# Merge gates of a streaming encoder layer: dense tiles, or pairs in seven quarter products added up in DRAM

## The chip, the cores and the metric

The kernel runs on one core of a Trainium2 chip. The metric is the device time of one launch in microseconds (us). One launch does one layer for a prompt of 1024 frames and a sample of 32 frames; the two are laid side by side, so that most operations work on T = 1056 columns.

## The reference, cut to what matters

```
h = rms(x);  z = h @ w_in, split into [q,k,v,r of the linear attention (GLA) | q,k,v of the band attention | gates gA, gB]
A = GLA(q, k, v) -> per-head rmsnorm, * silu(r), @ w_br_a          (4 heads)
B = softmax attention over a band of chunks, @ w_br_b              (8 heads)
mix = (sigmoid(gA)*A + sigmoid(gB)*B) @ w_out;   x += rms(mix)
x += rms(ConvFFN(rms(x)));   x += rms(sigmoid(rms(x) @ w_ple_gate) * (p @ w_ple))
```

The change concerns `z = h @ w_in`, with 1024 rows of h (the features) and 6672 columns of z. A *tile* is 128 of these columns: `Q0, K0, V0, R0` are the first tiles of the linear attention's q, k, v, r, `QB0, KB0, VB0` those of the band's, `GA0` and `GB0` those of the merge gates (8 tiles each). A tile's result has 128 partitions and T columns.

## The kernel before

Everything is kept in float32 accuracy by splitting each operand into a high and a low part (`whi`, `wlo` for weights, `xh`, `xl` for the normed input, 8 blocks of 128 rows each). A product of two such operands is three matmuls per block: high by high, high by low, low by high.

There are two ways to compute tiles of z. A *dense* tile is done in three chunks of 352 columns, 24 matmuls each, so 72 matmuls of 128x352. A *pair* of tiles in `in_strassen` takes the 2 by 2 form of Strassen and Winograd: the weights of both tiles are cut into quarters of four blocks, the input into quarters of four blocks by half of T (`one`, `two`), and seven quarter products replace eight. Each quarter product is 24 matmuls of 128x264, so a pair is 168 of them. It needs sums of weight quarters (made on VectorE) and sums of input quarters, named `t1` to `t4`, which were split into tiles `th` and `tl` at the start and live in SBUF until the stage of pairs ends.

The stages of the program, in order: start and norms; the stage of pairs (10 pairs: r, gB, and the first half of gA); the band attention; a short change-over; the linear attention in 16 steps `u` (4 heads by 4 segments); then the branch products, FFN and the rest, which the change touches only in where gates get their sigmoid. Inside the attentions the dense tiles that are left (`tiles`, 29 of them) are *fill*: TensorE has little work of its own there, so the code puts `piece()` between its steps. A piece is a third of a chunk, 8 matmuls on average. `flush()` writes the evacuations of finished chunks (PSUM to SBUF on ScalarE), `split_half` splits the next weights. TensorE, VectorE and ScalarE run in the written order (`manual_schedule`); on the DMA queues of SP and POOL a scheduler sets the order.

In the linear attention PSUM gives two banks to `mm` (fill) and six to `one`. A step turns the keys (`key_turns`, `key_copies`), forms products on six levels, masks them into `scores`, turns these (`score_turn` writes `turned`), updates the state, makes the outputs, and normalises them one step later (`roots`, `output_copies`, `output_turns`). `weight_sum` and `branch_sum` let POOL's queue add weight quarters of later stages in DRAM: a one-element DMA as a marker, a copy, and an accumulating DMA.

## Time and profile before

| what | before |
|---|---|
| median of 3 runs | 1871.55 us (1870.84 to 1872.83) |
| the profiled execution: its time / span of its records | 1871.93 / 1870.2 us |
| TensorE (PE) busy | 1841.6 us, 98% |
| VectorE (DVE) / ScalarE (ACT) / GpSimd (POOL) busy | 1287.3 / 976.9 / 227.7 us |
| stage of pairs | 81.7 to 287 us |
| band attention, change-over | 287 to 591 us |
| linear attention, up to its last step | 591 to 845 us |
| moved by DMA | 337.08 MB |

The profile is one execution. Matmuls are pipelined, so their recorded durations overlap, and an engine's busy time is the union of them. The pace of TensorE is therefore read from the distance of successive starts, not from the durations. A line such as `L822` is a line of the kernel's source.

### The profile page before, as it was taken

The page shows a single profiled execution, that of the slowest core. Times are in us where ns is not written, and L with a number is a line of the kernel's source. Part 1 is how long each engine was busy: PE and PEld are TensorE (multiplying, and loading weights), DVE is VectorE, ACT ScalarE, POOL GpSimd, SP SyncE. Part 2 cuts the span into 40 slices and gives each one's busy share as a digit, 9 for nine tenths or more (in the row PEclk, how much of TensorE's full clock was granted, in tenths as well). Part 3 has the DMA queues.
Part 4 walks back from the last instruction along what each step waited for, and adds up shares of the span by engine and source line. Part 5 has one row for each costly group of instructions (what it writes and reads, how often), then busy time and mean ns, then how long its engine had stood idle before and what let it go on. Part 6 is the DMA issues. An engine that isn't in the chain of part 4 may idle for free.

```text
span 1870.2 us, 35172 instructions
## 1 busy us (share of the span) xinstructions
PE 1841.6 (98%) x13808; PEld 1805.7 (97%) x13808; DVE 1287.3 (69%) x2427; ACT 976.9 (52%) x2062; POOL 227.7 (12%) x426
## 2 busy tenths in 40 slices
PE   8999999999999999999999999999999999999997
PEld 8999999999999999999999999999999999999996
DVE  6955543656655766766847776888888875568776
ACT  7545334666666676653536455433333345555555
POOL 0000001131100111100010121112122211000112
PEclk9999999999999999999999999999999999999998
DMA  7222326355434656678685477554566679887746
GB/s 283 85 104 100 120 81 198 96 142 139 118 84 123 163 151 181 165 213 268 235 252 174 155 266 283 169 177 169 182 183 172 166 212 303 287 273 248 234 150 111
DMA packets 129905, 337.08 MB, mean 180 GB/s; under 512 B 15236, under 2 KB 40652, under 8 KB 129100
## 3 DMA queue, kind: packets, MB, share of 16 engines
q1 hardware_dynamic: 93020, 221.82, 36.0%
q0 software_dynamic: 35280, 108.34, 22.0%
q10 hardware_dynamic: 1440, 4.69, 0.6%
q8 instruction: 108, 1.77, 0.4%
q14 instruction: 57, 0.47, 0.1%
HBM read 226.53 MB, written 133.29 MB: 192 GB/s over the span
## 4 chain that ended last, share of the span: by engine, by line
PE 85%; DVE 5%; ACT 4%; DMA 4%; issue 2%; SPq 0%; ACTq 0%; DVEq 0%
PE two L2387 6%; PE two L2385 6%; PE two L2386 6%; PE mm L822 5%; PE mm L824 5%; PE mm L823 5%; PE two L617 4%; PE two L618 4%; PE two L619 4%; PE mm L229 3%; PE mm L231 3%; PE mm L230 3%; PE two L2832 3%; PE two L2830 3%; PE two L2831 3%
## 5 line engine op out<-in xcount | busy, mean ns | idle before, releaser
L822 PE MATMUL mm<-xh,whi 128*128 128x352 f32 x696 | 240.5, 346 | 0.8 <-ACT ev L713 0.8
L824 PE MATMUL mm<-xh,wlo 128*128 128x352 f32 x696 | 225.0, 323 | 0.0
L823 PE MATMUL mm<-xl,whi 128*128 128x352 f32 x696 | 224.6, 323 | 0.0
L2832 PE MATMUL two<-d,wlo 128*128 128x264 f32 x616 | 174.4, 283 | 1.3 <-DVE wlo L2566 1.3
L2831 PE MATMUL two<-d,whi 128*128 128x264 f32 x616 | 174.7, 284 | 0.2 <-DVE d L2517 0.2
L2830 PE MATMUL two<-d,whi 128*128 128x264 f32 x616 | 174.6, 284 | 0.0
L2375 ACT ACTIVATE whi<-ws 128x512 fp32r<-128x512 f32 x88 | 55.5, 632 | 161.7 <-PE two L2386 160.7
L822 PEld LDWEIGHTS mm<-xh,whi 128*128 128x128 f32 x696 | 131.1, 188 | 3.3 <-ACT ev L713 1.1
L823 PEld LDWEIGHTS mm<-xl,whi 128*128 128x128 f32 x696 | 131.4, 189 | 0.0
L824 PEld LDWEIGHTS mm<-xh,wlo 128*128 128x128 f32 x696 | 130.6, 188 | 0.0
L2386 PE MATMUL two<-ml,whi 128*128 128x264 f32 x448 | 126.5, 283 | 0.0
L2387 PE MATMUL two<-mh,wlo 128*128 128x264 f32 x448 | 125.9, 284 | 0.0
L2385 PE MATMUL two<-mh,whi 128*128 128x264 f32 x448 | 125.8, 283 | 0.0
L2832 PEld LDWEIGHTS two<-d,wlo 128*128 128x128 f32 x616 | 116.4, 189 | 1.8 <-DVE wlo L2566 1.8
L2831 PEld LDWEIGHTS two<-d,whi 128*128 128x128 f32 x616 | 115.8, 188 | 0.5 <-DVE d L2517 0.5
L2830 PEld LDWEIGHTS two<-d,whi 128*128 128x128 f32 x616 | 115.7, 188 | 0.0
L235 DVE TENSOR_TENSOR wlo<-raw,whi 128x512 fp32r<-128x512 f32 x80 | 54.7, 688 | 59.3 <-ACT whi L234 58.8
L618 PE MATMUL two<-tl,whi 128*128 128x264 f32 x320 | 90.8, 284 | 0.0
L617 PE MATMUL two<-th,whi 128*128 128x264 f32 x320 | 90.8, 284 | 0.0
L619 PE MATMUL two<-th,wlo 128*128 128x264 f32 x320 | 90.6, 284 | 0.0
L2566 DVE TENSOR_TENSOR wlo<-wraw,whi 128x512 fp32r<-128x512 f32 (+1 forms) x81 | 51.7, 644 | 50.1 <-ACT whi L2565 50.0
L2386 PEld LDWEIGHTS two<-ml,whi 128*128 128x128 f32 x448 | 84.2, 188 | 0.0
(778 smaller groups left out, 6267.1 us busy)
## 6 DMA issues: line engine op xcount, KB each, us to landing
raw<-in_w_in SPq DMA_DIRECT2D x52, 512.0 KB, 3.7
d_b<-av POOLq DMA_DIRECT2D x33, 528.0 KB, 3.4
d_ws<-in_w_down POOLq DMA_DIRECT2D x24, 704.0 KB, 6.6
uraw<-d_b SPq DMA_DIRECT2D x32, 528.0 KB, 5.8
raw<-in_w_up SPq DMA_DIRECT2D x29, 512.0 KB, 4.6
sraw<-in_w_up SPq DMA_DIRECT2D x22, 512.0 KB, 3.6
wraw<-d_ws SPq DMA_DIRECT2D x16, 704.0 KB, 6.0
d_b<-sm POOLq DMA_DIRECT2D x11, 792.0 KB, 6.0
```

What stands on the lines that cost most here:

```text
L617: pe.matmul(ps[:, j, :HC], w[0][:, k], x[0](k, s), start=st, stop=False, skip_group_check=True)
L618: pe.matmul(ps[:, j, :HC], w[0][:, k], x[1](k, s), start=False, stop=False, skip_group_check=True)
L619: pe.matmul(ps[:, j, :HC], w[1][:, k], x[0](k, s), start=False, stop=sp_, skip_group_check=True)
L822: pe.matmul(ps, wh, h[:, k, s], start=(k == 0), stop=False)
L823: pe.matmul(ps, wh, l[:, k, s], start=False, stop=False)
L824: pe.matmul(ps, wl, h[:, k, s], start=False, stop=(k == cnt - 1))
L2385: pe.matmul(ps[:, j, :HC], w[0][:, k], x[0][:, k, s], start=st, stop=False, skip_group_check=True)
L2386: pe.matmul(ps[:, j, :HC], w[0][:, k], x[1][:, k, s], start=False, stop=False, skip_group_check=True)
L2387: pe.matmul(ps[:, j, :HC], w[1][:, k], x[0][:, k, s], start=False, stop=sp_, skip_group_check=True)
L2830: pe.matmul(o, wh, xh_[:, s], start=(k == 0 and p in (0, 4, 5)), stop=False, skip_group_check=True)
L2831: pe.matmul(o, wh, xl_[:, s], start=False, stop=False, skip_group_check=True)
L2832: pe.matmul(o, wl, xh_[:, s], start=False, stop=(k == HD - 1 and p in (3, 4, 6)), skip_group_check=True)
```

## The change

It trades places. The 16 gate tiles leave the stage of pairs and the dense fill, and become fill of a new kind: 8 pairs (tile n with tile n+4, `GATES`) of seven quarter products each, one product at a time, inside the change-over and the linear attention. Ten pairs of other tiles take the vacated places in the stage of pairs: r as before, three of band k with v, one of two band q tiles, k with q and the two v tiles of head 0. Thirteen dense tiles are left.

A quarter product is half an `Item`: two pieces of 12 matmuls of 128x264. The half results are not joined in SBUF: ScalarE copies each from PSUM to a staging tile `fv`, and POOL's queue writes or adds it to the gates' rows in DRAM (`into`), 72 DMAs in all. In the chained items the second half goes on accumulating in the bank that was just copied out. Since the input sums no longer fit in SBUF, they are stored to DRAM during the stage of pairs (`sum_store`) and later loaded over quarters of `xh`/`xl` that are no longer needed (`place`). The weight sums of the gates are made in DRAM too (`gate_sum`, 32 of them). The sigmoid of the gates moves to where they are read; for the tiles n below 4 the second half is stored with the opposite sign, so its sigmoid has scale -1.

Further: results of dense tiles and of the new pairs go through DRAM and are loaded where they are used (`band_row`, `head_value`, `head`); `weight_sum` moves from the linear attention to the band attention, and the accumulating DMAs of both sums are held back by two places (`second_sum`); the low halves of weights are written after the next piece begins (`lows`), `tidy` writes all evacuations but the last before each piece; `score_turn` moves ahead of two groups of exponentials; the pieces are spread by counts (`BAND_PIECES`, `GLA_FIRST`, `slot`) instead of `need`.

The core of the diff:

```diff
+BAND_PIECES = 120
+GLA_FIRST = 126
...
+    def gate_sum(n, at):
+        p, i = divmod(n, 4)
+        o = d_gs[p, i]
+        po.dma_start(o[0:1, 0, 0:1], at)
+        po.dma_start(o, (gate_quarter(p, 1, 0), d_gs[p, 0], gate_quarter(p, 0, 0), d_gs[p, 1])[i])
+        po.dma_start(o, gate_quarter(p, *((1, 1), (0, 0), (1, 0), (0, 1))[i]), accum_op=ALU.add)
...
     for n in range(0, 8, 2):
         in_strassen(R0 + n, R0 + n + 1, AF.Silu, d_sr[n], d_sr[n + 1], G_GLA + n)
-    for w0, d, top in ((GB0, d_gb, 8), (GA0, d_ga, GA_DENSE)):
-        for n in range(0, top, 2):
-            in_strassen(w0 + n, w0 + n + 1, AF.Sigmoid, d[n], d[n + 1])
+    for hp in (1, 2, 3):
+        in_strassen(KB0 + hp, VB0 + hp, None, d_bt[hp, 0], d_bt[hp, 2], keep=hp)
+    in_strassen(QB0 + 1, QB0 + 2, None, d_bt[1, 1], d_bt[2, 1], scale=(0.125, 0.125))
+    in_strassen(K0, Q0, None, d_kq[0, 0], d_kq[0, 1], scale=(1.0, QS))
+    in_strassen(V0, V0 + 1, None, d_v[0], d_v[1])
...
-    tiles = gate_tiles[:1] + [t for hp in (1, 2, 3) for t in band_tiles(hp)] + head_tiles(0) + gate_tiles[1:2]
-    tiles += [t for h in (1, 2, 3) for t in head_tiles(h)] + gate_tiles[2:]
+    tiles = [(QB0 + 3, keeper(d_bt[3, 1], 0.125))]
+    for h in (1, 2, 3):
+        tiles += [(K0 + h, keeper(d_kq[h, 0], 1.0)), (Q0 + h, keeper(d_kq[h, 1], QS))]
+        tiles += [(V0 + 2 * h + j, keeper(d_v[2 * h + j], 1.0)) for j in range(2)]
+    for p in range(0, 8, 2):
+        tiles.append(Item(False, *[(gate_quarter(q, 0, 1), 1, Q21, 1.0, into(False, (GATES[q][2], one))) for q in (p, p + 1)]))
+    for p, (n1, n2, z1, z2) in enumerate(GATES):
+        tiles.append(Item(True, (gate_quarter(p, 0, 0), -1, Q11, -1.0, into(True, (z1, one))),
+                          (d_gs[p, 1], 1, Q12, 1.0, into(False, (z2, one), (z2, two), (z1, two)))))
...
+    def item_parts(i, c):
+        half, j = divmod(c, 2)
...
+        if not (half and x.chain):
+            fill["banks"][j] = ps_mm()[:, :HC]
+        ps = fill["banks"][j]
...
+        def evac():
+            if j == 0:
+                fill["stage"] = stage_tile()
+            t = fill["stage"]
+            ac.activation(t[:, j * HC : (j + 1) * HC], ps, AF.Copy, scale=scale)
+            if j:
+                store(t)
```

Three places in the program show what stands in the engines' rows. In the rows a name with a number is one buffer, `out<-in` its operands, and a wait names the engine or DMA lane whose semaphore is awaited.

TensorE, in the step of the linear attention that begins head 1, ahead of the state update (`kt` are the turned keys, `whi` and `wlo` split weights, `mm` the fill's bank, `ot` the outputs of the step ahead). Before:

```order
L822 MATMUL mm_7783<-xh_111,whi_7638 128x352
L823 MATMUL mm_7783<-xl_112,whi_7638 128x352
L824 MATMUL mm_7783<-xh_111,wlo_7639 128x352
L1375 MATMUL one_7811<-vt_6951,kt_7806 128x256 [waits PE_49,Activation_49]
L1375 MATMUL one_7811<-vt_6951,kt_7806 128x256
L1320 MATMUL one_7727<-x_7570 128x128 [waits DVE_49]
L1320 MATMUL one_7728<-x_7570 128x128 [waits DVE_49]
L1462 MATMUL one_7825<-ident_78,ot_7735 128x128 [waits Activation_49]
```

The same place after:

```order
L1440 MATMUL one_8073<-x_7906 128x128 x2
L859 MATMUL mm_8108<-xh_108,whi_8058 128x264 [waits Activation_49]
L860 MATMUL mm_8108<-xl_109,whi_8058 128x264
L861 MATMUL mm_8108<-xh_108,wlo_8059 128x264 [waits DVE_49]
```

The fill ahead of the update is now the second half of a chained item: its first matmul waits for ScalarE, which must have copied out the same bank, and its third for VectorE's low part of the weights.

ScalarE at the same place, from the turned keys on (`fv` is a staging tile, `kq` the keys and queries of the next head). Before:

```order
L1343 ACTIVATE kt_7806<-one_7731 128x256
L1455 ACTIVATE ot_7735<-one_7717,rs_7760 128x256 [waits DVE_49]
L1455 ACTIVATE ot_7735<-one_7717,rs_7760 128x256
L1455 ACTIVATE ot_7735<-one_7605,rs_7760 32x256
L742 ACTIVATE kq_7764<-mm_7783 128x256 [waits DMAHW1_49,DMAHW0_49,PE_49]
L742 ACTIVATE kq_7764<-mm_7783 128x96
L1261 ACTIVATE x_7770<-x_7770 128x64x2 [waits DMASW4_49,DVE_49]
```

After:

```order
L867 ACTIVATE fv_8131<-mm_8108 128x264 [waits DMASW7_49,PE_49]
L867 ACTIVATE fv_8131<-mm_8136 128x264 [waits PE_49]
L1340 ACTIVATE vt_7158<-one_8162 128x512 [waits PE_49]
L817 ACTIVATE whi_8182<-raw_7916 128x512 [waits DMAHW2_49]
L1465 ACTIVATE kt_8185<-one_8077 128x256
L1577 ACTIVATE ot_8081<-one_8063,rs_8127 128x256 [waits DVE_49]
L1577 ACTIVATE ot_8081<-one_8063,rs_8127 128x256
L1577 ACTIVATE ot_8081<-one_7942,rs_8127 32x256
L867 ACTIVATE fv_8230<-mm_8108 128x264 [waits DMASW1_49,DMASW2_49,DMASW0_49,PE_49]
L867 ACTIVATE fv_8230<-mm_8136 128x264 [waits PE_49]
```

Two evacuations of an item and a weight split stand ahead of the keys' copy, two more evacuations behind it, and an evacuation waits for POOL's DMAs (the lanes DMASW) that last read its staging tile.

POOL in the linear attention (`d_ws` and `d_gb` are in DRAM). Before:

```order
L1490 DMA d_ws_6827<-x_7570 1x1 [waits DMASW0_49,DVE_49,Activation_49]
L1491 DMA d_ws_6827<-d_ws_6827 16x11264 [waits DMASW0_49]
L1492 DMA d_ws_6827<-in_w_down 128x1408 [waits DMASW1_49]
L1490 DMA d_ws_6827<-x_7770 1x1 [waits DMASW3_49,DVE_49,Activation_49]
L1491 DMA d_ws_6827<-d_ws_6827 16x11264 [waits DMASW3_49]
```

After:

```order
L748 DMA d_gb_964<-fv_7433 128x528 [waits DMASW1_49,Activation_49]
L748 DMA d_gb_964<-fv_7498 128x528 [waits DMASW2_49,Activation_49]
L748 DMA d_gb_964<-fv_7498 128x528 [waits DMASW3_49]
L748 DMA d_gb_964<-fv_7498 128x528 [waits DMASW4_49]
L774 DMA xl_109<-fv_7569 1x1 [waits DMASW5_49,Activation_49]
L748 DMA d_gb_964<-fv_7569 128x528 [waits Activation_49]
L775 DMA xl_109<-d_t_960 128x4x528 [waits DMASW7_49,DMASW5_49]
```

Where the queue added weights of a later stage, it now stores the gates' quarter products, and loads the input sums behind a marker; the weight sums stand in the band attention's rows.

More of the change, by code (lines that the diff above doesn't have):

```diff
@@ L182, in width @@
         return CHUNKS[c][1] - CHUNKS[c][0]
-    def rstd(s, rows=P):
-        c, a = next((c, a) for c, (a, b) in enumerate(CHUNKS) if a <= s.start and s.stop <= b)
-        return rstds[c][:rows, s.start - a : s.stop - a]
     convst = tl(cst, [P, FT, 2], tag="convst")
@@ L807, in times_gate @@
         return evac
+    def item_parts(i, c):
+        half, j = divmod(c, 2)
+        x, (src, sign, (rows, cols), scale, store) = tiles[i], tiles[i].halves[half]
+        h, l = [t[half] for t in fill["w"][i]]
+        if not (half and x.chain):
+            fill["banks"][j] = ps_mm()[:, :HC]
+        ps = fill["banks"][j]
+        s = slice(cols.start + j * HC, cols.start + (j + 1) * HC)
+        for k in range(HK):
+            b = rows.start + k
+            pe.matmul(ps, h[:, k], xh[:, b, s], start=(k == 0 and not (half and x.chain)), stop=False, skip_group_check=True)
+            pe.matmul(ps, h[:, k], xl[:, b, s], start=False, stop=False, skip_group_check=True)
+            pe.matmul(ps, l[:, k], xh[:, b, s], start=False, stop=(k == HK - 1), skip_group_check=True)
+        def evac():
[5 more added lines that the diff above has]
+                store(t)
+        fill["done"].append(evac)
+        yield
     def unit_parts(i, c):
+        if isinstance(tiles[i], Item):
+            yield from item_parts(i, c)
+            return
         hi, lo = fill["w"][i]
@@ L1517, in emit @@
     head(1)
-    while fill["at"] < 3 * 15 + 1:
+    while fill["n"] < GLA_FIRST:
         piece()
@@ L1542, in steps_of, with slot @@
             f()
-    need = [fill["at"] + n / 30 for n in range(82, 82 * 12 + 1, 82)]
-    need += [3 * FIRST - (3 * FIRST - need[-1]) * n / 3 for n in (2, 1)]
+    slots = [0]
+    def slot(k=1):
+        for i in range(k):
+            slots[0] += 1
+            if OB.get("h") is not None or fill["n"] < min(MAIN, GLA_FIRST + (MAIN - GLA_FIRST) * slots[0] / (9 * 14.7)):
+                piece()
     level_start(0)
@@ L1643, in emit @@
             gate_rows(1)
+        if u == 15:
+            log_exp()
         roots(u)
-        if u < 14 and fill["at"] + (fill["now"] or (0, 0))[1] / 3 < need[u]:
-            piece()
+        flush()
+        if u < 15:
+            gates(u)
+        if u < 14:
+            slot()
         if u == 13:
```

322 lines of the change are left out of this document (197 added, 125 removed).

## The prediction

> **What bounds the kernel now.** I read the page's engines first, then the stages by windows, then who TensorE waits for, and last the pace of its matmuls.
>
> ```profile
> PE 1841.6 (98%) x13808; PEld 1805.7 (97%) x13808; DVE 1287.3 (69%) x2427; ACT 976.9 (52%) x2062; POOL 227.7 (12%) x426
> PE 85%; DVE 5%; ACT 4%; DMA 4%; issue 2%; SPq 0%; ACTq 0%; DVEq 0%
> ```
>
> TensorE is busy for 98% of the span and carries 85% of the chain that ended last. By stage (columns: length, then busy time and count of PE, weight loads, DVE, ACT, POOL, then granted clock, DMA share, GB/s):
>
> ```profile
> 81.70:287.00 205.30, 204.55 (x1680) 204.34 (x1680) 110.42 (x163) 88.91 (x122) 1.09 (x6) 1.00 0.29 99
> 313.00:575.00 262.00, 258.04 (x1779) 246.08 (x1779) 156.79 (x386) 167.29 (x403) 39.57 (x90) 1.00 0.44 112
> 575.00:592.00 17.00, 17.00 (x114) 16.74 (x114) 6.98 (x22) 11.99 (x41) 0.27 (x1) 1.00 0.48 151
> 592.00:852.00 260.00, 259.56 (x1647) 245.30 (x1646) 183.37 (x541) 165.61 (x605) 30.72 (x53) 1.00 0.64 176
> 852.00:881.00 29.00, 28.23 (x169) 26.06 (x168) 17.20 (x48) 10.09 (x27) 0.83 (x1) 1.00 0.82 257
> 881.00:986.00 105.00, 105.00 (x817) 104.84 (x815) 74.32 (x119) 47.30 (x80) 5.12 (x6) 1.00 0.78 251
> ```
>
> These are the pairs, the band attention, the change-over, the linear attention, its end and the branch stage. No stage leaves TensorE idle by more than 4 us at full clock, so time falls where matmul columns fall, as long as the other engines keep up. Who it waits for from 287 to 592 us, then from 592 to 905 us (total us, times, longest):
>
> ```profile
> PE two L954 <- DVE sm L960: 1.9, 4, 0.6
> PE one L967 <- ACT s L961: 1.3, 8, 0.2
> PE mm L822 <- ACT ev L713: 0.8, 1, 0.8
> PE one L1008 <- DVE pt L970: 0.7, 1, 0.7
> PE mm L822 <- DVE ev L804: 0.6, 1, 0.6
> PE one L1219 <- ACT ev L713: 0.4, 1, 0.4
> ```
>
> That is 4.7 us in 14 waits, 0.34 us each, and then 1.0 us: the fill covers nearly every delay of the attentions.
>
> **Fewer columns.** The pace of matmuls by successive starts, first of the pairs (35 starts in this stretch), then of dense fill (96 starts):
>
> ```profile
> 199.80 0.29 PE L619 MATMUL two<-xh,wlo 128*128 128x264 f32 x1
> 203.94 0.28 PE L617 MATMUL two<-th,whi 128*128 128x264 f32 x1
> 287.12 0.32 PE L822 MATMUL mm<-xh,whi 128*128 128x352 f32 x1
> 302.55 0.32 PE L824 MATMUL mm<-xh,wlo 128*128 128x352 f32 x1
> ```
>
> 4.14 us over 34 steps is 0.1218 us for 264 columns; 15.43 us over 95 is 0.1624 us for 352. Sixteen dense tiles' worth of work leaves: 16 x 72 x 0.1624 = 187.1 us. Eight pairs come: 8 x 168 x 0.1218 = 163.7 us. The stage of pairs keeps its ten pairs. So TensorE sheds **23.4 us**, all of it fill. By place: up to the linear attention there were 46 chunks of 24 matmuls (179.3 us) and will be 13 tiles and 9 of the new pieces (152.0 + 13.2 = 165.2 us), 14.1 us less; in the linear attention 41 chunks (159.8 us) become 103 pieces of 12 x 0.1218 = 1.46 us (150.5 us), 9.3 us less.
>
> The Trainium skill speaks against this: TensorE: Matmul & The Clock Gate, section Back-to-back issue gap, gives for a sustained stream of weight loads and matmuls about 81 ns at 128 columns and 131 ns at 512, so narrow matmuls pay more per column. An estimate on a straight line between these is 99 ns at 264 and 110 ns at 352; by it a pair costs 16.6 us against 15.9 us for two dense tiles, and the change would add 5.7 us instead of taking 23.4. The rows above decide otherwise: 0.1218 to 0.1624 is as 264 to 352 in both widths, so I give that outcome no chance.
>
> **More work for ScalarE and VectorE in the linear attention.**
>
> ```profile
> L234 ACT ACTIVATE whi<-raw 128x512 fp32r<-128x512 f32 x80 | 49.5, 623 | 16.2 <-PE mm L823 8.9 <-PE two L618 7.2
> L713 ACT ACTIVATE ev<-mm 128x352 f32<-128x352 f32 x69 | 31.3, 454 | 23.7 <-PE mm L824 22.1 <-issue 1.1
> L1343 ACT ACTIVATE kt<-one 128x256 f32<-128x256 f32 x16 | 6.0, 377 | 0.5 <-PE one L1338 0.5
> L235 DVE TENSOR_TENSOR wlo<-raw,whi 128x512 fp32r<-128x512 f32 x80 | 54.7, 688 | 59.3 <-ACT whi L234 58.8
> 650.80:669.00 18.20, 18.20 (x112) 16.52 (x111) 12.10 (x36) 8.91 (x34) 1.90 (x3) 1.00 0.53 136
> 669.00:686.00 17.00, 17.00 (x113) 16.53 (x111) 11.07 (x32) 14.37 (x49) 1.88 (x3) 1.00 0.56 150
> 686.00:703.20 17.20, 17.20 (x113) 16.75 (x111) 12.78 (x40) 11.30 (x44) 1.90 (x3) 1.00 0.54 146
> L1297 PE MATMUL one<-kq x72: 206/326/430, 590.9 to 845.2; 128*128 128x192 f32 x64, 128*32 128x48 f32 x8
> ```
>
> A dense tile costs ScalarE two weight splits and three evacuations, 2 x 0.623 + 3 x 0.454 = 2.61 us. An item, with half a tile's matmuls, costs two splits and four evacuations of 264 columns; the nearest row for those is the keys' copy, 0.377 us: 2.75 us. In the linear attention 13.67 tiles (35.7 us) become 25.75 items (70.9 us): ScalarE rises from 165.6 to about 201 us of a stage that would last 251, 80%. VectorE gains 2 x 0.688 us for each item more: 183.4 + 16.6 = 200 us, 80% too. The last row gives the first and last step's start: 15 steps in 254.3 us, 16.95 us each. The three rows above it are steps of the second head; the fullest has 14.37 us of ScalarE, and with 35.2 / 15 = 2.3 us more it holds 16.7 us, against a step that should shrink by 9.3 / 15 to 16.3. So the throughput just holds in most steps, but the margins go. One of the rows shown above goes with it: a wait of 0.34 us. I take one such wait in each of 16 steps, **+5.4 us**. Bounds: 0 (ScalarE still idles 50 us there, and `score_turn` now stands ahead of exponentials), and 16 us, half a ScalarE split and evacuation (0.5 of 1.0 us) twice in each step.
>
> **The change-over.** From 575 to 592 us there were 27 dense first matmuls (81 in all, 13.2 us); now 6 new pieces, 8.8 us. So 4.4 of the 23.4 us shed lie here, and could leave 12.6 us, which ScalarE's 11.99 us nearly fill. Here the cover goes, and the exponentials of the first step are late next. I take a third as not won, **+1.5 us** (0 to 4.4).
>
> **Sigmoids.** Eight gate rows more get theirs after the pairs.
>
> ```profile
> L1797 ACT ACTIVATE ev<-ev 128x1056 f32<-128x1056 f32 x4 | 4.3, 1082 | 1.3 <-DMA ev<-d_ga 1.3
> L652 ACT ACT_TABLE_LOAD x2 | 2.6, 1283 | 0.3 <-DVE ev L651 0.3
> 859.30 0.28 ACT L1330 ACTIVATE turned<-one 128x128 f32<-128x128 f32 x1 [4.51 <-PE one L1329]
> 875.00 0.63 ACT L234 ACTIVATE whi<-raw 128x512 fp32r<-128x512 f32 x1 [7.00 <-PE mm L823]
> ```
>
> Four stand in the last step: 4 x 1.08 us and two table loads of 1.28 us, 6.9 us on ScalarE, where it idled 4.5 us at the last step's turn and 7.0 us after. One load stands ahead of the last `roots`, which the output turns wait for: **+0.5 us** (0 to 2.6). The others lie beside the branch stage, where ScalarE is busy for 47 of 105 us: 0 (to 1).
>
> **DMAs and their queues.** POOL's list grows by 174 rows, SP's by 88.
>
> ```profile
> q1 hardware_dynamic: 93020, 221.82, 36.0%
> q0 software_dynamic: 35280, 108.34, 22.0%
> raw<-in_w_in SPq DMA_DIRECT2D x52, 512.0 KB, 3.7
> d_tb<-ev POOLq DMA_DIRECT2D x6, 528.0 KB, 7.8
> gw<-d_gate POOLq DMA_DIRECT2D x4, 1024.0 KB, 11.1
> 712.07 0.84 POOL L1492 DMA_DIRECT2D d_ws<-in_w_down  x1 [5.01 <-DMA d_ws<-d_ws]
> POOL bias L895 <- DMA bias<-in_rel: 122.0, 7, 29.5
> ```
>
> POOL moved 108.34 MB in 22% of the span, 411 us of all engines, 263 MB per ms. In the stage of pairs, 32 weight sums of two times 256 KB and 16 stores of 528 KB are 25 MB, 96 us: the share goes from 0.29 to about 0.76. Weights land in 3.7 us and are asked for a pair (20.5 us) ahead, so 0 (to 3). In the band attention 16 weight sums move in, 32 x 704 KB or 23 MB, 88 us of 250, and about 12 MB of stores and loads of q, k, v at SP's 329 MB per ms, 36 us: 0.44 becomes 0.94. POOL's `bias` fills (L895) stand behind these sums; POOL waited 122 us there for data and has a whole half-head, 262 / 8 = 33 us, to be late. **+1 us** (0 to 6). In the linear attention 72 gate stores need an issue of 0.84 us each in 250 us, and an accumulating store of twice their size lands in 7.8 us while a staging tile is free for three others; a sum's load takes 11.1 us and is issued at least 9 pieces (20 us) ahead: 0 (to 3).
>
> **Sum**: -23.4 + 5.4 + 1.5 + 0.5 + 1.0 = -15.0 us against the execution's own 1871.9 us, which is 0.4 us above the median: 1856.9, and 1856.5 against the median. With all low ends: 1848. A change of 0.2%, 3.7 us, is about what a measurement can tell from none.
>
> **The rivals.**
> - *All of it hidden* (0.14): ScalarE's 50 us of slack and the new order cover every delay; even some of the 4.7 us before the linear attention may go. 1848. For it: TensorE waited 1.0 us there before. Against: 80% occupancy on two in-order engines.
> - *ScalarE sets the steps* (0.13): the upper bound of that term, 16 us, eats most of the gain: 1871.5 - 23.4 + 16 + 3 = 1867, so half of it lies within 0.2%. For it: 16.7 us of ScalarE in a step of 16.3. Against: the steps beside the full one have 8.9 and 11.3 us, so what is late can be caught up.
> - *The two banks* (0.08): this one ends slower. Each half of a chained item adds to the bank that ScalarE has just copied out, with one other piece between; before, a bank rested for three pieces. With the other 3 us of cost, the gain of 23.4 is gone if the 112 new pieces wait 0.18 us each; with one split (0.62) and an evacuation (0.38) ahead at every third piece the mean is 0.33 us, 37 us in all: 1871.5 - 23.4 + 37 + 3 = 1888. For it: six instructions stand between two evacuations in ScalarE's new rows. Against: the own work of the linear attention stands between most pieces. The Trainium skill, Perfetto Trace Analysis, section Matmuls, asks for independent groups to rotate through different banks so that an evacuation overlaps the next group; no run so far shows its price here.
> - *DMA in the band attention* (0.05): at a share of 0.94 the band's own loads come late, say 4 us in each of 7 half-heads: 1871.5 - 15 + 28 = 1884. Against: the branch stage runs at 0.78 without a wait.
> - Two of these at once (0.02): slower.
>
> **How the numbers follow.** The forecast's case has 0.58 and reaches by itself from 1849 to 1864, the term of waits at 0 or 13 us. The predicted time is 1856.5. From 1847 to 1872 hold this case, most of the hidden one and the one of ScalarE, 0.83. Faster by over 0.2%: 0.58 + 0.14 + half of 0.13, 0.78; within: the other half, 0.07; slower: 0.08 + 0.05 + 0.02 = 0.15.
>
> **What will show it.** The new fill's matmuls at 0.122 us from start to start; the stage of pairs within 2 us of 205; the linear attention's 15 steps at 16.3 to 16.8 us each; ScalarE near 200 us there. Waits of fill on `fv` of more than 0.2 us a piece would show the two banks; waits of L954's successor on DMAs the band. It would be wrong if the steps stayed at 17 us, which I would see as waits on ScalarE's splits or evacuations.

## The result, and the profile after

The change made the kernel slower: 1897.9 us median (1889.7 to 1902.5, 4 runs) against 1871.2 us for the kernel before beside it, a ratio of 1.0138 (95% interval 1.0102 to 1.0174). The forecast was 1856.5 us.

The profiled execution took 1898.3 us, its span is 1896.4 us, 26.2 us more than the span before. Three rows per kernel say where. The first start of the row `one<-kq` is the start of the linear attention, its last start that of the last step; the first weight sum of the FFN (`ws<-sraw`) comes after the branch stage. The row `one<-kq` of before stands in the prediction (590.9 to 845.2); these are the sum of before, and both rows of after:

```profile
L2368 DVE TENSOR_TENSOR ws<-sraw x22: 683/684/694, 1170.9 to 1490.3; 128x512 f32<-128x512 f32 x22
```

```profile
L1417 PE MATMUL one<-kq x72: 206/326/401, 610.2 to 867.0; 128*128 128x192 f32 x64, 128*32 128x48 f32 x8
...
L2504 DVE TENSOR_TENSOR ws<-sraw x22: 684/688/694, 1196.9 to 1516.2; 128x512 f32<-128x512 f32 x22
```

| part | before | after | change | forecast |
|---|---|---|---|---|
| up to the linear attention | 590.9 | 610.2 | +19.3 | -14.1 + 1.5 + 1.0 = -11.6 |
| its 15 steps | 254.3 | 256.8 | +2.5 | -9.3 + 5.4 = -3.9 |
| last step to the FFN's first weights | 325.7 | 329.9 | +4.2 | +0.5 |
| the rest | 699.3 | 699.5 | +0.2 | 0 |
| sum | 1870.2 | 1896.4 | +26.2 | -15.0 |

Of the 41.2 us between forecast and result, 30.9 lie ahead of the linear attention, 6.4 in its steps, 3.7 behind them. Windows of after (columns as in the prediction: length, busy time and count of PE, weight loads, DVE, ACT, POOL, then granted clock, DMA share, GB/s), for the pairs, the band and the linear attention:

```profile
81.70:286.90 205.20, 204.50 (x1681) 204.29 (x1682) 110.35 (x163) 80.23 (x115) 79.47 (x127) 1.00 0.80 228
313.00:575.00 262.00, 236.62 (x1601) 225.86 (x1600) 143.22 (x354) 153.87 (x372) 68.63 (x136) 0.95 0.85 231
610.20:867.00 256.80, 251.48 (x1876) 235.95 (x1875) 191.92 (x553) 187.15 (x648) 59.75 (x88) 1.00 0.87 236
```

In the stage of pairs the DMA share went from 0.29 to 0.80 and TensorE did not notice: 205.2 us against 205.3. In the band attention it went from 0.44 to 0.85, and TensorE is idle for 25 us of the same 262, where it was idle for 4. Who it waited for from 287 to 610 us:

```profile
PE one L1188 <- DMA qs<-d_alr: 14.7, 1, 14.7
PE two L1035 <- DVE sm L1041: 8.6, 5, 5.3
PE mm L859 <- ACT fv L867: 2.2, 2, 1.4
PE mm L890 <- ACT fv L734: 2.0, 1, 2.0
```

Two of these waits, 14.7 and 5.3 us, are most of it. The first is for the low-rank input of the gates (`qs<-d_alr`), which `decays` asks for through POOL's queue. POOL's timeline shows when it got there (start, duration of the issue, in brackets what it waited for before):

```profile
544.71 0.56 POOL L1139 DMA_DIRECT2D d_wa<-in_w_br_a  x1 [19.59 <-DMA d_wa<-sums]
545.26 0.50 POOL L1155 DMA_DIRECT2D d_ws<-d_ws  x1
549.77 0.83 POOL L1132 DMA_DIRECT2D d_wa<-in_w_br_a  x1 [4.01 <-DMA d_wa<-in_w_br_a]
551.27 0.84 POOL L1132 DMA_DIRECT2D d_ws<-in_w_down  x1 [0.66 <-DMA d_ws<-d_ws]
551.80 0.86 POOL L1183 DMA_DIRECT2D qs<-d_alr  x1
```

The load is issued at 551.8 us, behind the last weight sums, on a queue that had just stood 19.6 us for a marker of one element. In the kernel before it was issued at 536.8 us and landed in 3.8 us, here in 9.8; so 15 us of its lateness come from the queue's order and 6 from its own landing. TensorE stands from 547 to 561.8 us. The other wait starts on SP's queue and ScalarE:

```profile
514.48 0.30 SPq L1175 DMA_DIRECT2D d_inv<-ot  x1
```

```profile
536.64 0.38 ACT L1055 ACTIVATE ot<-one 64x256 f32<-64x256 f32 x1 [6.65 <-DMA d_inv<-ot]
```

A store of 9 KB, issued at 514.5 us, let its tile go 22 us later; ScalarE stood in order for that tile, the scores' exponentials behind it, VectorE behind these, TensorE behind VectorE. Behind both stand late landings, seen in the DMA issues from 286 to 592 us (KB of each, median us from issue to landing), before and after:

```profile
raw<-in_w_in SPq DMA_DIRECT2D x15, 512.0 KB, 3.6
bias<-in_rel SPq DMA_DIRECT2D x8, 336.0 KB, 2.8
d_wa<-sums POOLq DMA_DIRECT2D x16, 0.0 KB, 1.5
```

```profile
d_ws<-in_w_down POOLq DMA_DIRECT2D x24, 704.0 KB, 15.0
raw<-in_w_in SPq DMA_DIRECT2D x10, 512.0 KB, 14.9
bias<-in_rel SPq DMA_DIRECT2D x8, 336.0 KB, 11.0
d_wa<-sums POOLq DMA_DIRECT2D x16, 0.0 KB, 12.2
```

These three land four to eight times later, on SP's queue as on POOL's; most others land 1.5 to some three times later (`kl<-kl` 8.3 and 12.2 us, `kh<-kh` 4.2 and 8.6, `d_ob<-ev` 4.0 and 13.0). (The Trainium skill, DMA: Bandwidth & Descriptors, section Queues, rings and completion order, says that each DMA engine takes packets in turn from all queues that have work for it; SP's loads slowed by POOL's sums agree with that.)

The idle stretches cost a second time here, in TensorE's clock. The same windows of before, then of after, at the start of the band; then after, around the two long waits:

```profile
300.00:305.00 5.00, 4.22 (x26) 3.93 (x25) 1.54 (x3) 2.92 (x6) 0.00 (x0) 1.00 0.67 249
305.00:310.00 5.00, 5.00 (x35) 4.42 (x34) 4.30 (x8) 2.95 (x7) 0.00 (x0) 1.00 1.03 271
```

```profile
300.00:305.00 5.00, 3.05 (x19) 2.76 (x18) 1.33 (x3) 2.08 (x5) 0.29 (x2) 1.00 0.86 334
305.00:310.00 5.00, 5.00 (x24) 4.50 (x23) 3.89 (x6) 2.92 (x5) 0.00 (x0) 0.55 0.93 231
538.00:545.00 7.00, 5.99 (x28) 5.72 (x29) 1.88 (x7) 2.02 (x7) 0.29 (x1) 0.54 1.04 306
555.00:560.00 5.00, 0.00 (x0) 0.00 (x0) 0.00 (x0) 0.00 (x0) 0.00 (x0) 0.50 0.92 210
560.00:565.00 5.00, 3.24 (x12) 3.20 (x12) 0.00 (x0) 1.00 (x2) 0.00 (x0) 0.50 0.26 54
565.00:570.00 5.00, 5.00 (x23) 4.71 (x24) 2.08 (x7) 3.17 (x9) 0.00 (x0) 0.67 0.10 36
```

From 305 to 310 us TensorE is "busy" for 5.00 us in both, with 35 matmuls before and 24 after: the clock is 0.55. By an estimate from these rows, half clock costs 0.45 x 5 + 0.46 x 6 + 0.5 x 3.2 + 0.33 x 5 = 8 us, beside some 26 us more of waits (30.6 us from 287 to 610 us against 4.7). Together that is about the 19.3 us and the 14.1 us of columns that went.

### The profile page after: what moved, and what is told of

Read it like the earlier page. It is cut to its first block, busy times and chain, and to the rows that moved or that the text cites. A ratio compares the mean times of both kernels' runs of the same rounds, so it can differ in the third digit from the quotient of the medians.

```text
span 1896.4 us, 36233 instructions
## 1 busy us (share of the span) xinstructions
PE 1831.3 (97%) x14000; PEld 1791.7 (94%) x14000; DVE 1301.3 (69%) x2451; ACT 1005.1 (53%) x2126; POOL 369.0 (19%) x641
## 4 chain that ended last, share of the span: by engine, by line
PE 56%; DVE 4%; ACT 4%; DMA 3%; issue 1%; SPq 1%; DVEq 0%; ACTq 0%; POOLq 0%
PE two L2523 6%; PE two L2521 6%; PE two L2522 6%; PE mm L228 3%; PE mm L226 3%; PE mm L227 3%; PE two L2968 3%; PE two L2966 3%; PE two L2967 3%; PE mm L859 2%; PE mm L860 2%; PE mm L861 2%; PE two L2430 1%; PE two L2432 1%; PE two L2431 1%
## 5 line engine op out<-in xcount | busy, mean ns | idle before, releaser
L859 PE MATMUL mm<-xh,whi 128*128 128x264 f32 x448 | 134.8, 301 | 3.7 <-ACT fv L867 3.6
L860 PE MATMUL mm<-xl,whi 128*128 128x264 f32 x448 | 127.4, 284 | 0.0
L861 PE MATMUL mm<-xh,wlo 128*128 128x264 f32 x448 | 127.2, 284 | 0.0
L890 PE MATMUL mm<-xh,whi 128*128 128x352 f32 x312 | 111.0, 356 | 2.0 <-ACT fv L734 2.0
L892 PE MATMUL mm<-xh,wlo 128*128 128x352 f32 x312 | 103.0, 330 | 0.0
L891 PE MATMUL mm<-xl,whi 128*128 128x352 f32 x312 | 102.8, 330 | 0.0
L859 PEld LDWEIGHTS mm<-xh,whi 128*128 128x128 f32 x448 | 84.9, 190 | 5.6 <-ACT fv L867 5.0
L860 PEld LDWEIGHTS mm<-xl,whi 128*128 128x128 f32 x448 | 84.5, 189 | 0.0
```

The source lines that it names most:

```text
L859: pe.matmul(ps, h[:, k], xh[:, b, s], start=(k == 0 and not (half and x.chain)), stop=False, skip_group_check=True)
L860: pe.matmul(ps, h[:, k], xl[:, b, s], start=False, stop=False, skip_group_check=True)
L861: pe.matmul(ps, l[:, k], xh[:, b, s], start=False, stop=(k == HK - 1), skip_group_check=True)
L890: pe.matmul(ps, wh, h[:, k, s], start=(k == 0), stop=False)
L891: pe.matmul(ps, wh, l[:, k, s], start=False, stop=False)
L892: pe.matmul(ps, wl, h[:, k, s], start=False, stop=(k == cnt - 1))
```

## The experiments

All times of stages are from one profiled execution of each kernel; ratios are to the kernel before, run beside it. The starts in this table are those of the weight loads of `one<-kq`, 0.1 to 0.2 us ahead of its matmuls, and the FFN's first stage is counted from its first weight sum (`ws<-sraw`) to its last (`ws<-raw,sraw`). A profiled execution can lie well off its median: 1874.4 us in e1, 1891.2 in e2, 1871.3 in e4, 1879.9 in e9.

| run | linear attention starts | its 15 steps | to FFN | FFN's first stage | median us (lowest, highest) | ratio, 95% interval |
|---|---|---|---|---|---|---|
| before | 590.8 | 254.4 | 325.7 | 338.7 | 1871.2 | |
| after | 610.1 | 256.9 | 329.9 | 338.5 | 1897.9 (1889.7, 1902.5) | 1.0138 [1.0102, 1.0174] |
| e1 | 587.2 | 257.1 | 328.8 | 338.5 | 1878.7 (1874.4, 1886.1) | 1.0040 [1.0023, 1.0058] |
| e2 | 582.9 | 254.7 | 329.6 | 362.1 | 1886.7 (1882.1, 1891.2) | 1.0073 [1.0055, 1.0091] |
| e3 | 582.0 | 280.6 | 331.8 | 338.5 | 1898.1 (1894.7, 1905.9) | 1.0148 [1.0120, 1.0175] |
| e4 | 591.1 | 254.4 | 324.8 | 338.7 | 1879.3 (1870.5, 1881.4) | 1.0030 [1.0016, 1.0044] |
| e5 | 582.2 | 255.9 | 329.4 | 353.1 | 1885.5 (1881.8, 1892.1) | 1.0084 [1.0058, 1.0110] |
| e6 | 582.9 | 253.0 | 329.0 | 356.4 | 1884.6 (1884.2, 1885.0) | 1.0069 [1.0049, 1.0090] |
| e7 | 580.7 | 254.5 | 328.8 | 353.7 | 1881.3 (1880.6, 1885.5) | 1.0058 [1.0041, 1.0075] |
| e8 | 583.0 | 251.1 | 329.3 | 351.6 | 1877.4 (1877.1, 1883.1) | 1.0041 [1.0025, 1.0057] |
| e9 | 594.1 | 254.3 | 330.6 | 338.6 | 1876.6 (1874.5, 1882.5) | 1.0032 [1.0022, 1.0041] |
| e10 | 595.8 | 255.0 | 325.7 | 338.5 | 1877.7 (1876.0, 1881.3) | 1.0034 [1.0021, 1.0047] |
| e11 | 583.2 | 256.7 | 329.5 | 342.6 | 1871.4 (1866.7, 1879.6) | 1.0000 [0.9989, 1.0011] |
| e12 | 585.1 | 257.1 | 327.5 | 338.5 | 1872.4 (1864.9, 1875.9) | 0.9999 [0.9985, 1.0013] |
| e13 | 584.1 | 260.5 | 326.1 | 338.6 | 1870.7 (1867.3, 1876.4) | 0.9996 [0.9987, 1.0005] |
| e14 | 584.5 | 255.5 | 327.1 | 338.5 | 1867.6 (1865.6, 1871.9) | 0.9975 [0.9962, 0.9989] |

**The band attention: e1 to e4, and e9.** Theory "volume": the weight sums fill the DMA engines, all data come late, and it costs where an engine in order stands at a late tile. Rivals: "queue" (only what stands behind the sums on POOL's queue) and "elsewhere".

e1, one load on another queue:

```diff
-        po.dma_start(alr, d_alr)
+        if h:
+            po.dma_start(alr, d_alr)
+        else:
+            dma.dma_start(alr.bitcast(F32), d_alr.bitcast(F32))
```

> The changed kernel, but the first load of the gates' low-rank input (qs<-d_alr) goes through SP's queue instead of POOL's, where it stood behind the weight sums. Theory 'volume': the weight sums fill the DMA engines in the band attention, so everything asked for there lands late. Then this load is asked for at about 532 us, lands in some 15 us like the weights, and the wait of 14.7 us goes with about 4 us of half clock behind it; the wait of 5.3 us at 533 us (behind the store d_inv, 22 us to land on SP's queue) and the slow start of the stage stay: 1898 - 19 = 1879 us. Rival 'queue': only what stands behind the sums on POOL's queue is late, and the rest follows from it: 1898 - 26 = 1872 us. Rival 'elsewhere' (the engines' new work, not DMAs): no change, 1898 us.

1878.7 us, 19.2 less than the changed kernel, as "volume" had it; the longest wait for `sm` stayed at 4.1 us. One moved load is half of what the forecast missed. The moved load itself stood behind the sums on POOL's queue, so this half is a wait of that queue by either theory; what speaks against "queue" is that 7 us stayed.

e2, the sums in the FFN's first stage (`weight_sum` in `up_strassen` instead of `band`):

```diff
-                if n < 16:
-                    weight_sum(*divmod(n, 4), B[hp]["sums"][hd][0:1, 0:1])
...
+        if f < 16:
+            weight_sum(*divmod(f, 4), q[0:1, 0, 0:1])
```

> The changed kernel, with the 16 weight sums taken out of the band attention and made in the first stage of the FFN, one for each of its first 16 steps; everything else as in the changed kernel. Volume: the band's mean DMA share falls from 0.84 to about 0.5, its loads land in 4 to 6 us again, and its waits fall from 31 us to about 6: 1898 - 26 = 1872 us, or a few us less. Queue: the same here. Elsewhere: 1898 us. The FFN's stage has a DMA share of 0.5 to 0.7 and gets 0.3 more: 0 to 3 us.

In the band it did what was expected: the linear attention starts 27.2 us earlier. The band's window, and the landing times from 286 to 592 us, are now:

```profile
313.00:575.00 262.00, 252.98 (x1766) 241.62 (x1764) 158.66 (x397) 171.22 (x420) 41.36 (x92) 1.00 0.56 157
```
```profile
raw<-in_w_in SPq DMA_DIRECT2D x10, 512.0 KB, 5.7
...
d_wa<-sums POOLq DMA_DIRECT2D x16, 0.0 KB, 1.6
```

But the FFN's stage, put at 0 to 3 us, lost 23.4 (362.1 us against 338.7 before). The rows there are the waits of POOL, SP's queue, VectorE and TensorE:

```profile
POOL d_ws L1155 <- DMA d_ws<-c: 104.7, 16, 8.1
```
```profile
SPq L2578 <- DMA d_b<-av: 54.3, 8, 11.4
```
```profile
DVE ws L2500 <- DMA sraw<-in_w_up: 28.0, 8, 5.4
```
```profile
PE two L2517 <- DVE av L2576: 14.3, 5, 4.7
```

POOL stood 6.5 us for each marker in order, its stores of `av` behind it. SP's queue stood 54.3 us for these stores (3.3 us in the changed kernel), and VectorE 28.0 us for weights that come by SP's queue and 16.5 us for stores of `sm`; the changed kernel's list has neither of the two. This stage is as dense as that of the pairs, and its DMA share of 0.81 was not free. A wait on a queue is paid by what is queued behind it, which is the mechanism of e1 in another stage.

e3, the sums back in the linear attention:

```diff
+        weight_sum(h, s, X[u][0:1, 0, 0:1])
+        while later:
+            second_sum()
         flush()
         loads(u)
```

> The changed kernel, with the 16 weight sums back in the linear attention, one at the start of each step, as before the change. Volume: the band attention gets its 26 us back, but the linear attention's DMA share of 0.87 would have to go to 1.2, so it becomes late there: 10 to 30 us longer, 1882 to 1902 us in all. Queue: the gates' stores stand behind the sums, evacuations wait for staging tiles, some 5 us: 1877 us. If neither volume nor queue matters in the linear attention: 1872 us.

The size is that of "volume": the band is as in e2, and the linear attention, now with a share of 1.01, takes 280.6 us. Its window, and the waits of TensorE and of ScalarE:

```profile
582.00:862.60 280.60, 260.04 (x1876) 241.33 (x1874) 191.84 (x553) 187.63 (x647) 87.76 (x128) 0.98 1.01 286
```

```profile
PE mm L859 <- ACT fv L867: 9.8, 7, 3.5
PE one L1517 <- DVE turned L1449: 5.0, 3, 4.0
PE one L1493 <- ACT kt L1461: 3.0, 2, 2.0
```
```profile
ACT fv L867 <- DMA d_gb<-fv: 15.0, 4, 5.8
ACT fv L867 <- DMA d_ga<-fv: 10.3, 3, 4.6
```

The way it is paid is in part that of "queue": TensorE's longest wait, on `fv`, stands behind 25.3 us that ScalarE waited for staging tiles, whose stores stood behind the sums on POOL's queue. Weights came late too: `raw<-d_gs` on SP's queue landed in 9.1 us against 5.1 in e2. This run doesn't separate the two.

Beside the change's own stores the sums could not stay where they were.

e4, the kernel before with the sums in the band and `second_sum` (the diff is the change's own lines for these two):

> The kernel before, with one part of the change alone: the 16 weight sums made in the band attention, and the accumulating DMAs of both sums held back by two places. The band's DMA share goes from 0.44 to about 0.75. Volume: this is below what hurts (a stage at 0.78 had no waits), so at most 5 us slower: 1871 to 1876 us. Queue: the low-rank input stands behind the sums on POOL's queue as in the changed kernel and comes late by about 15 us: 1886 to 1890 us. Elsewhere: 1871 us.

+5.6 us over the kernel before by the ratio's middle and +7.7 by the medians, over the upper end of "volume" and well below "queue". In its profile the band's share is 0.77, weights land in 8.8 us, biases in 8.7 and markers in 6.0, and yet TensorE waits no more than before, 0.6 us of it for `qs<-d_alr`: late landings alone cost nothing there. But its runs lie from 1870.5 to 1881.4 us and the profiled one took 1871.3, so where the others lost is not shown. The same sums on the same queue cost about a quarter of what they cost in the changed kernel, where the band moves other new data as well.

e9, after e1 also the tile of the other long wait:

```diff
-        inv = tl(bp, [P, 256], tag="ot", bufs=2)[:9]
-        ac.activation(inv, ps[:9, : 2 * P], AF.Copy)
-        dma.dma_start(d_inv[hp].rearrange("h (n q) -> n h q", q=P), inv.rearrange("n (h q) -> n h q", q=P))
+        inv = tl(bp, [P, P], tag="inv", bufs=1)
+        for hd in range(2):
+            t = inv[32 * hd : 32 * hd + 9]
+            ac.activation(t, ps[:9, hd * P : hd * P + P], AF.Copy)
+            dma.dma_start(d_inv[hp, hd].rearrange("(n q) -> n q", q=P), t)
```

> The changed kernel with the weight sums still in the band attention. The low-rank input is loaded through SP's queue, as in the first experiment, and the sums of the softmax that are stored to d_inv get a tile of their own instead of a turn of the tag ot, so that the outputs' copies no longer wait for that store to land. Volume theory (all that is asked for in the band lands late, but it costs only where TensorE has no fill left or an engine in order stands at the late tile): the wait of 5.3 us at 533 us and some 3 us of half clock behind it go too, 1878.7 - 6 = 1872 us (1868 to 1876). Rival: the late data show up at the next thing that is asked for (biases, rows of the next head), and the time stays at 1878 us.

The time is nearer the rival's than the theory's. The wait for `d_inv` is gone, and in the profiled execution (1879.9 us) two others stand in its place:

```profile
PE two L1036 <- DMA kl<-kl: 3.3, 1, 3.3
...
PE one L1193 <- DMA qs<-d_alr: 1.8, 1, 1.8
```

1876.6 us against 1878.7 in e1, with ratios whose intervals overlap: no gain is shown, and with the volume unchanged the next late tile pays.

**The linear attention: e5 to e8.** e5 is the base: e2 with each sum spread over three FFN steps.

```diff
+        if f < 16:
+            po.dma_start(d_ws[f // 4, f % 4, 0:1, 0:1], at)
+        if 1 <= f < 17:
+            i, m = divmod(f - 1, 4)
+            po.dma_start(d_ws[i, m], WSUMS[i][0][m])
+        if 2 <= f < 18:
+            i, m = divmod(f - 2, 4)
+            po.dma_start(d_ws[i, m], WSUMS[i][1][m], accum_op=ALU.add)
```

> The changed kernel with the weight sums in the first stage of the FFN as before, but spread over three steps each: marker in one step, copy in the next, accumulating DMA in the one after, so that POOL's queue need not stand waiting for each to land while its own copies and stores of that stage wait behind. Volume theory (the band's loss is DMA volume; the 23 us that the FFN's stage lost in the run before are POOL's waits for markers of 6.5 us and copies of 4.5 us): the FFN's stage loses at most half of that, 0 to 12 us, and the whole is 1867 to 1879 us, the attentions as in the run before (583 and 255 us). Rival: the DMA share of 0.8 itself slows that stage (weights late): it stays at 362 us and the whole at 1887 us.

The FFN's stage lost 14.4 us instead of 23.4: less, and more than the 12 allowed. The scheduler of POOL's queue put most copies right behind their markers again, so the edit was only half made. As a base for the steps it serves: 255.9 us.

e6 leaves out the accumulating stores (40 of the 72; the expectation's 48 was a miscount), e7 every other evacuation of the items, e8 their low halves:

```diff
-            for d, h in places:
+            for d, h in places if not acc else ():
```
```diff
             t = fill["stage"]
+            if j == 0:
+                return
```
```diff
-            pe.matmul(ps, l[:, k], xh[:, b, s], start=False, stop=(k == HK - 1), skip_group_check=True)
+            pe.matmul(ps, h[:, k], xh[:, b, s], start=False, stop=(k == HK - 1), skip_group_check=True)
```

> The same, and of the gates' stores the accumulating ones are left out (48 of 72), so the gates' rows hold only part of their sums. In the linear attention 15 steps took 254.7 us with clean bands, though 6.9 us of fill columns went; so about 7 us of stalls came in. Theory 'DMA': the linear attention's share of 0.88 makes weights and loads late, and a store holds its staging tile too long; with a share near 0.6 the 15 steps take 248 to 250 us. Theories 'ScalarE', 'VectorE' and 'latency' (the own work's chain from engine to engine, with less fill in each step to cover it): 253 to 255 us.

> As the first of these, and ScalarE copies only the second 264 columns of each staging tile, which are stored twice; half of the items' evacuations, 52 x 0.37 us or 19 us of ScalarE, are left out. Theory 'ScalarE' (splits and evacuations stand ahead of the step's own copies): the 15 steps take 248 to 251 us. DMA, VectorE, latency: 253 to 255 us.

> As the first of these, and the low half of the items' weights isn't made: the third matmul of each block takes the high half, so its product is wrong; VectorE has 51 x 0.69 us, 35 us less to do, and no matmul waits for a low half. Theory 'VectorE': the 15 steps take 248 to 251 us. ScalarE, DMA, latency: 253 to 255 us.

The windows from 583 to 838 us of e5, e6, e7, e8 show what each took away (DMA share 0.87 to 0.63; ScalarE 187.6 to 173.5 us; VectorE 191.2 to 166.9):

```profile
583.00:838.00 255.00, 250.40 (x1870) 235.40 (x1868) 191.19 (x551) 187.62 (x648) 59.36 (x86) 1.00 0.87 236
```
```profile
583.00:838.00 255.00, 252.63 (x1888) 237.65 (x1886) 194.07 (x559) 188.77 (x654) 25.50 (x48) 1.00 0.63 199
```
```profile
583.00:838.00 255.00, 250.70 (x1873) 235.38 (x1871) 193.60 (x557) 173.51 (x602) 79.04 (x87) 1.00 0.91 240
```
```profile
583.00:838.00 255.00, 253.81 (x1904) 238.84 (x1902) 166.90 (x511) 189.99 (x657) 60.89 (x88) 1.00 0.88 241
```

The steps took 253.0, 254.5 and 251.1 us. Kernels with the same code there took 254.3 to 257.1 (after, e1, e2, e5, e9, e10), so e7 cannot be told from none, e6 is 1.3 us below the lowest of them and above what "DMA" had forecast (248 to 250), and e8 is clear, 4.8 us below its base and 3.2 below the lowest; the waits for `scores` fell from 1.9 to 0.5 us in it. No single engine held all of the 7 us that these steps lost: VectorE's low halves are the largest part; whether DMA has one is not shown by a single execution; and ScalarE, which the forecast looked at, has none that shows.

**The end of the linear attention: e10.** VectorE's and ScalarE's order in the last step and in the branch stage:

```diff
         if u == 15:
+            score_last(u)
             gates(u)
...
-            if (n, c) in ((4, 1), (6, 1)):
-                sigmoid(gb[n + 1], gb[n + 1], n + 1)
+            if (n, c) in ((4, 1), (7, 0)):
+                sigmoid(gb[n | 1], gb[n | 1], n | 1)
```

> The same, and two things in another order at the end of the linear attention: in its last step VectorE's score_last stands ahead of the branch's splits instead of behind them, and the sigmoid of the last gate row stands at its use, so that ScalarE doesn't stop in order at a row that is still loading. From the last step's start to the FFN's first weights it took 329.9 us (before: 325.7, though 2.4 us of fill went). Theory 'order': the wait of 1.3 us for turned, the 2 us of half clock behind it and most of the 1.6 us for half go: 325 to 327 us, the whole 3 to 5 us less than the run beside it. Rival 'latency' (the last step has no other fill to cover its chain): 329 us, no change.

325.7 us, as "order" had it, and the waits for `turned` and `half` are gone from this stage. The whole did not follow: this run's band started the linear attention at 595.8 us (`kl` 5.5 us late). In e11 to e14, with the same two edits, the stretch took 326.1 to 329.5 us, against 328.8 to 330.6 in the kernels without them (after, e1, e2, e5 to e9). The wait for `turned` stays away in all five, so the first edit holds; `half` waits again in e11, e12 and e14, 1.3 to 1.8 us, so the second was not enough. The two are worth some 2 us on the average. Half clock is not what they save each time: behind the same wait of 1.3 us the clock was 0.95 in the changed kernel and 1.00 in e5 and e9.

**Without the cause: e11 to e14.** All have the edits of e1, e9 and e10. e11 makes eight sums in the band, eight in the FFN. e12 makes the first four while the norms run, twelve in the band; e13 four, eight and four.

```diff
+    def early_sums():
+        at = ys[two.start][0:1, 0:1]
+        for m in range(4):
+            po.dma_start(d_ws[0, m, 0:1, 0:1], at)
+        for k in range(2):
+            for m in range(4):
+                po.dma_start(d_ws[0, m], WSUMS[0][k][m], **({"accum_op": ALU.add} if k else {}))
```

> The same as the second, with the first 8 weight sums in the band attention (its first half) and the other 8 in the first stage of the FFN, spread over three steps each. Volume: the band's share falls from 0.84 to about 0.72 and its last third has none of the sums, so linear attention starts at 582 to 586 us; the FFN's stage pays half of the 23 us that all sums cost there or less, 3 to 7 us: 1866 to 1872 us. If the cost of the sums in the FFN's stage is one of its first steps alone: 1875 us or more.

> The changed kernel with the low-rank input on SP's queue, the d_inv tile of its own and the two things in another order at the end of the linear attention, as two runs before; and the weight sums stand elsewhere. The first four, which need only inputs, are made from 47 to 80 us, while the norms run: the DMA share there is 0.01 to 0.45 and POOL's queue is empty. The other twelve are made in the band attention's second to fifth half-heads, so its last third, where the late data cost 20 us, has none. Volume: linear attention starts at 582 to 586 us, as with eight sums in the FFN, and no stage pays for it elsewhere: 1871.4 - 4 = 1867 us (1864 to 1871). Rival 'total': the band's share of 1.0 from 330 to 460 us makes data late there, and the start is at 590 us or more: 1874 us.

> The same, with eight sums in the band attention's second to fourth half-heads and the last four in the first stage of the FFN, each spread over three of its first nine steps. Volume: the band as with eight sums (583 us), and the FFN's stage pays 0 to 2 us instead of 4: 1868 us (1865 to 1871). If it is faster than the run beside it by 3 us or more, twelve sums are still too many for the band; if it is slower, the FFN's steps pay for each sum.

The linear attention starts at 583 to 585 us in all three, as "volume" said, and the early sums cost nothing that shows. The medians are that of the kernel before within 1.4 us: e11 and e13 lie in their ranges, e12 1.4 us above its own, with runs from 1864.9 to 1875.9. That e13's median lies 1.7 us below e12's is too little to say which split is better. What was left stood in one step, shown by e13 (ScalarE, then SP's queue):

```profile
737.77 0.63 ACT L835 ACTIVATE whi<-raw 128x512 fp32r<-128x512 f32 x1 [6.76 <-DMA raw<-d_gs]
```
```profile
731.66 2.70 SPq L1661 DMA_DIRECT2D vt<-d_inv  x4
734.41 1.57 SPq L805 DMA_DIRECT2D raw<-d_gs  x2
```

Four broadcast loads stand ahead of the item's weights; `turned` is behind the split in ScalarE's order, and TensorE waited 5.2 us for it. The changed kernel had the same wait, 1.7 us at 762. e14 is e12 with these loads held back by two one-column copies:

```diff
+        for o in (0, T):
+            ve.tensor_copy(r[:, o : o + 1], ident[:, 0:1])
         for k, t in enumerate(OB["t"]):
             dma.dma_start(t, d_ob[k])
```

> The same kernel as e12, with one thing more in the linear attention: two one-column copies on VectorE hold back the four broadcast loads vt<-d_inv (1 MB) until head 3, which SP's queue had taken forward into a step of head 2 ahead of the weights of the next item; there ScalarE stood 2.9 to 6.8 us for these weights, in order, with turned behind it. Theory 'late weights': that step loses its 1 to 5 us, the 15 steps take 253 to 255 us instead of 257 to 260 and the runs scatter less: 1869 us (1865 to 1871). Rival: with a share of 0.88 the loads delay the weights wherever they stand; the wait moves to head 3's first step and the time stays at 1872 us.

1867.6 us against 1872.3 for the kernel before beside it, 0.9975 [0.9962, 0.9989]: a version of the change that beats the kernel before, by 4.7 us. The wait for `turned` is gone, and the steps take 255.5 us against 257.1 in e12's profile. What the pin is worth by itself the times don't show: e12's interval (0.9985 to 1.0013) still touches this one. Whether the pin or the early sums would help the kernel before was not tried; its waits in the linear attention show no such stop.

## Why the prediction was wrong, step by step

- *Fewer columns, 23.4 us:* right. The new fill in a stretch of 24 matmuls of the linear attention:

```profile
626.47 0.29 PE L859 MATMUL mm<-xh,whi 128*128 128x264 f32 x1
...
629.28 0.28 PE L861 MATMUL mm<-xh,wlo 128*128 128x264 f32 x1
```

  2.81 us over 23 steps is 0.122 us. The estimate that the prediction worked out from the Trainium skill (TensorE: Matmul & The Clock Gate, section Back-to-back issue gap), 99 ns, does not hold here, and the outcome it gave had rightly no chance. The place was a little off: between the first and the last step's start there were 969 fill matmuls before (157.4 us) and 1236 after (150.5), 6.9 us less and not 9.3; the other 2.4 us lay in the last step.
- *DMAs and their queues, +1 us (0 to 6):* **the step that failed.** The volume was put at a share of 0.94 in the band and came out at 0.85 (SP's queue moved 36.1 MB from 286 to 592 us where it had moved 29.5, not 12 more); the bytes fitted and the inference from that was wrong. It priced the transfers by their own length, with a stage at 0.78 as proof that a high share is free. Measured: landing times of weights, biases and markers four to eight times longer, one load late by 14.7 us, one buffer by 6.7, and half clock behind both; with the sums out of the band (e2) the linear attention starts 27.2 us earlier, where the term had 1 us. The text saw `bias` as the thing behind the sums; it did not look for what else stood there, and `qs<-d_alr` did, at the band's end, where TensorE's written order had the dependent matmul and no fill ahead of it. The rival *DMA in the band attention* (28 us, 1884 us), with a chance of 0.05, named the stage and the cause. Its size came near by luck: it had 4 us in each of 7 half-heads, and 20.0 of the 30.6 us of waits are two waits at the band's end, with half clock on top.
- *Waits in the linear attention, +5.4 us:* the stage took 2.5 us more where 6.9 us of columns went: 9.4 us, inside the bounds of 0 to 16. TensorE waited 1.7 us for `turned`, 1.5 for `scores`, 1.4 for `fv`; the rest stands in no wait of that list, and its cause is open. The cause was misnamed: e8 finds 4.8 us with VectorE's low halves, the wait for `turned` stood behind late weights, and e7 finds nothing with ScalarE's copies (187 us busy, and not 201). The steps took 17.1 us each, which the prediction had named as the sign of being wrong, but with 1.4 us of waits on ScalarE's evacuations and none on its splits, which is not the cause that it tied to it.
- *Two banks:* not so. `fv` cost 3.6 us in all 112 pieces, 0.03 us a piece; the rival needed 0.18.
- *Change-over, +1.5 us:* not separable. Even with no sums in the band (e2, e3, e5 to e8) the linear attention starts at 581 to 583 us, and with some of them at 583 to 585 (e11 to e14), against a forecast of 579.3; the waits left there in e14 are `sm` 3.6, `fv` 2.5 and 2.2, `s` 1.6 and `sums` 1.2 us.
- *Sigmoids, +0.5 us:* too small. The end took 4.2 us more though 2.4 us of fill went. `score_last` behind the branch's splits, a row of gates in ScalarE's order and one half clock stand there; e10 took the 4.2 us back in its run, and e11 to e14 a part of them.
- *Pairs within 2 us of 205:* right, at a DMA share of 0.80.

Taken together in e14: 23.4 us of columns were shed and 3.8 us came out in the span (1866.4 against 1870.2). By the table, 7.8 of the other 19.6 us were lost ahead of the linear attention, 8.0 in its steps and 3.8 behind them; the waits named above hold a part of that, and the rest is open.

## What to carry to other kernels

A mean DMA share says whether a stage's bytes fit, not when a given one arrives. Here landing times grew up to eight times, on both queues, at a share of 0.85, and the price was set by the few tiles that an engine in order met with no work ahead of it. So where a change adds volume, list each small load, store and marker on each queue in that stage, multiply its landing time by four, and look who stands behind it; then look for a stretch where the DMA engines idle, as in the norms here. The share itself sets no price: 0.80 was free in the stage of pairs, 0.81 cost 23.4 us in the FFN's stage (e2), where stores and weights stood behind markers, and 0.85 cost 27.2 us in the band, whose steps depend on late loads.

## What the runs showed of the hardware

Half clock can follow a short idle. After 1.31 us of idle, 12 matmuls of 352 columns ran at 0.29 us from start to start instead of 0.16:

```profile
883.97 0.67 PE L1521 MATMUL one<-vt,turned 128*128 128x256 f32 x2 [1.31 <-DVE turned L1453]
...
886.64 0.50 PE L890 MATMUL mm<-bh,whi 128*128 128x352 f32 x1
886.93 0.50 PE L891 MATMUL mm<-bl,whi 128*128 128x352 f32 x1
```

After 1.95 us at 304 us it lasted for some 7 us, and after 2.49 us at the same place in e2 there was none, so the length of the idle alone does not decide it here. The Trainium skill, TensorE: Matmul & The Clock Gate, Part 1, puts the drop behind an idle window of about 3.4 us; it came after shorter ones here, and the measurement decides. A DMA of one element (`d_wa<-sums`) took 12.2 us in the median and up to 21.0 us to land in the band attention at a share of 0.85, against 1.5 us in the median before and 1.6 in e2.
